# Second layer's v chunks: the low part of every second weight tile made by an adding DMA instead of VectorE

## Chip, cores and metric

The kernel runs on one core of a Trainium2 chip. The metric is the device time of one execution in microseconds (us), the median of several executions. Smaller is better.

## What is computed

A two-layer decoder trunk on 256 positions of width 2048, in float32. The first layer is attention with an output projection; the second is a gated unit. The change sits in the second layer, whose input projection is the wide one (2048 x 12288, cut into u, v and gate of 4096 columns each):

```python
def _odd_layer(x, ln_g, w_in, v_g, w_s, b_s, w_out):
    h = _rms(x, ln_g)
    z = h @ w_in
    uv = gelu(z[..., :2 * C_WIDTH])
    gate = silu(z[..., 2 * C_WIDTH:])
    u, v = uv[..., :C_WIDTH], uv[..., C_WIDTH:]
    v = _rms(v, v_g).reshape(Bn, S // C_CHUNK, C_CHUNK, C_GROUPS, C_GROUP_DIM)
    ws = w_s * tril(ones)
    s = einsum('gts,bnsgc->bntgc', ws, v) + b_s.T[:, :, None]
    return x + (u * s.reshape(Bn, S, C_WIDTH) * gate) @ w_out
```

## The kernel before

**Split products.** Every big product is done with numbers split into two parts of type fp32r: a high part (the value rounded) and a low part (the value minus its high part). A product a x w becomes three matmuls: high x high (line 121), high a x low w (line 122), low a x high w (line 123).

**Weight tiles.** `wtile` (lines 75 to 88) brings one weight tile of 128 x 2 x 512 float32 (512 KB, two k tiles of 128 rows, one chunk of 512 columns). SyncE issues the load into `wraw` (line 80, six buffers). ScalarE copies it to `whi` (line 85, four buffers), which rounds it. VectorE subtracts, `wlo` = `wraw` - `whi` (line 86, four buffers). A buffer of `whi` or `wlo` is free again when TensorE has done the last matmul that reads it, so the tile that stands four places later takes it.

**Chunks.** `gemm` (lines 100 to 126) computes one chunk of 512 output columns for both halves of the 256 positions. For the input projection of the second layer it goes through 16 k tiles in eight weight tiles (k0 = 0, 2, ..., 14), and does twelve matmuls of 512 columns with each of them: six into the PSUM bank of the first 128 positions, then six into that of the second.

**The v chunks.** Lines 557 to 566 run eight chunks, the columns 8 to 15 of `w_in1`. After each chunk ScalarE evacuates two banks with a Gelu (line 191, in `evac`) and sums squares of both halves (line 562, `junk`). GpSimd fetches a piece of the gain (line 564, `gv`) and multiplies it onto the chunk (line 565, `v`). The next chunk's matmuls don't wait for any of that. Afterwards the u and gate chunks follow.

**Order.** The framework orders each engine's instructions from the dependencies and its own estimate of when each is ready; instructions that stand earlier in the program go first among those that are ready. Each engine then runs its list strictly in that order and waits on semaphores where data isn't there yet.

Of the kernel before, what the change touches and what calls it, by code (L numbers as in the profile page):

```python
# [10 lines left out]
F32 = mybir.dt.float32  # L11
# [3 lines left out]
ALU = mybir.AluOpType  # L15
# [5 lines left out]
KT = D // P  # L21
# [12 lines left out]
def trunk(ctx, tc, x, xT, ev_g, w_in0, w_kva, qk_g, sinks, w_out0, od_g, w_in1, v_g, w_sT, b_s,  # L34
          w_out1, bias, badd, tri, out):
    nc = tc.nc
# [16 lines left out]
    def nm(s):  # L53
        uid[0] += 1
        return f"{s}{uid[0]}"

    def psum(tag, bufs):
        return ps.tile([P, 512], F32, tag=tag, bufs=bufs, name=nm(tag))
# [13 lines left out]
        return y  # L72


    def wtile(w, kt, cw, fine=False):
        raw = wpool.tile([P, 2, 512], F32, tag="wraw", bufs=6, name=nm("wraw"))
        src = w[kt // 2].rearrange("p (k n) -> p k n", k=2)
        step = 1 if fine else 2
        for j in range(0, 2, step):
            nc.sync.dma_start(raw[:, j:j + step, :cw], src[:, j:j + step, :])  # L80
        hi = wpool.tile([P, 2, 512], F32R, tag="whi", name=nm("whi"))
        lo = wpool.tile([P, 2, 512], F32R, tag="wlo", name=nm("wlo"))
        for j in range(0, 2, step):
            js = slice(j, j + step)
            nc.scalar.copy(hi[:, js, :cw], raw[:, js, :cw])  # L85
            nc.vector.tensor_tensor(lo[:, js, :cw], raw[:, js, :cw], hi[:, js, :cw].bitcast(F32),  # L86
                                    op=ALU.subtract)
        return hi, lo
# [3 lines left out]
    def fill():  # L92
        while fillers:
            try:
                next(fillers[0])
                return
            except StopIteration:
                fillers.pop(0)

    def gemm(aT, nkt, w, cw, pre=None, last=False):  # L100

        acc = [(psum("g", 4), 0, 0, cw), (psum("g", 4), 1, 0, cw // 2 if last else cw)]
        if last:
            acc.append((psum("g", 4), 1, cw // 2, cw))
        for k0 in range(0, nkt, 2):
            if pre is not None:
                pre(k0)
            fine = pre is not None and k0 == 0  # L110
            whi, wlo = wtile(w, k0, cw, fine)
            work = [(g, k) for g in acc for k in range(2)]
            if fine:
                work.sort(key=lambda t: t[1])
            for n, ((bank, tt, a, b), k) in enumerate(work):
                kt = k0 + k
                ah, al = aT(kt)
                sl = slice(tt * P, (tt + 1) * P)
                st, en = kt == 0, kt == nkt - 1
                o = bank[:, :b - a]  # L120
                nc.tensor.matmul(o, ah[:, sl], whi[:, k, a:b], start=st, stop=False)  # L121
                nc.tensor.matmul(o, ah[:, sl], wlo[:, k, a:b], start=False, stop=False)  # L122
                nc.tensor.matmul(o, al[:, sl], whi[:, k, a:b], start=False, stop=en)  # L123
                if n % 2:
                    fill()
        return acc if last else [g[0] for g in acc]
# [264 lines left out]
    def gate_y(q, y, gate):  # L391
# [3 lines left out]
        yield from split_T(y, yT0, q, [("t", 1)])  # L395

    in0 = lambda c, pre=None: gemm(hTk, KT, w_in0[c], 512, pre)

    acc = in0(QA, load_hT)
# [22 lines left out]
    zq1 = evac(accq, 512, rs=rs, name="qa")  # L422
    qk_norm(zq)
    acc1 = gemm(hTk, KT, w_kva, 256)
    qkg = cons.tile([P, 4], F32, name="qkg")
    nc.scalar.dma_start(qkg, qk_g)
# [70 lines left out]
    hT1 = [None] * 4  # L497
    ss1 = cons.tile([P, 2, 4], F32, name="ss1")

    def yTk(yT):  # L500
        def get(kt):
            while yT[kt // 4] is None:
                fill()
            return yT[kt // 4][0][:, kt % 4, :], yT[kt // 4][1][:, kt % 4, :]
        return get
# [29 lines left out]
    for q in range(4):  # L535
        acc = gemm(yTk(yT0), KT, w_out0[q], 512)
        resid(q, acc)
        fillers.append(next_hT(q))
# [12 lines left out]
        nc.gpsimd.tensor_tensor(t, t, trit.unsqueeze(1).broadcast_to([P, 8, P]), op=ALU.mult)  # L551
        ws.append(t)

    in1 = lambda c: gemm(yTk(hT1), KT, w_in1[c], 512)
    ssv = cons.tile([P, 2, 8], F32, name="ssv")
    vt = []
    for c in range(8):
# [132 lines left out]
```

## Time and profile before

| | |
|---|---|
| median of 3 runs | 1171.48 us (1170.75 to 1171.59) |
| the profiled execution | 1171.01 us |
| its span in the trace | 1169.2 us |
| TensorE busy in the span | 1162.0 us, 99% |
| VectorE busy | 647.5 us, 55% |
| ScalarE busy | 595.2 us, 51% |
| GpSimd busy | 135.7 us, 12% |
| DMA | 218.37 MB, mean 187 GB/s |

The trace has one row for each instruction: when it started, how long it ran, and what ended the idle time of its engine before it. PE is TensorE, ACT is ScalarE, DVE is VectorE, POOL is GpSimd, SP is SyncE, which issues most DMAs. A matmul's row is 0.39 us long, but matmuls overlap in the array: one starts every 0.227 us. The v chunks lie between about 449 and 625 us of the span.

### The profile page before, as it was taken

How to read it: one execution, taken by the hardware profiler on the slowest of the kernel's cores; microseconds unless marked ns; L12 is line 12 of the kernel's file. 1: busy time of each engine (PE TensorE's matmuls, PEld its weight loads, DVE VectorE, ACT ScalarE, POOL GpSimd, SP SyncE). 2: the span in 40 equal slices, each digit the busy share in tenths (PEclk: the TensorE clock that was granted, in tenths of full speed). 3: DMA queues.
4: the chain of work that ended last, by engine and by line, in shares of the span. 5: the costliest groups of instructions: out<-in, count | busy, mean ns of one | idle time of the engine just before them, and what ended most of it. 6: DMA issues, size and time to landing. Idle time of an engine off the chain costs nothing.

```text
span 1169.2 us, 14610 instructions
## 1 busy us (share of the span) xinstructions
PE 1162.0 (99%) x5546; PEld 963.0 (82%) x5546; DVE 647.5 (55%) x837; ACT 595.2 (51%) x818; POOL 135.7 (12%) x85
## 2 busy tenths in 40 slices
PE   9999999999999999999999999999999999999998
PEld 7887888788788888888888888888888888888887
DVE  6586556655645555554556555565556555454453
ACT  6556654544654544544545554555464455433332
POOL 0131111112103000211215110100000000000000
PEclk9999999999999999999999999999999999999999
DMA  9675335436436655666665555555555665566661
GB/s 349 232 245 195 127 108 184 172 109 208 160 123 219 196 186 183 203 212 200 202 213 178 184 188 190 181 178 187 186 187 171 190 187 173 198 215 199 200 213 37
DMA packets 63638, 218.37 MB, mean 187 GB/s; under 512 B 7632, under 2 KB 10320, under 8 KB 63312
## 3 DMA queue, kind: packets, MB, share of 16 engines
q1 hardware_dynamic: 60352, 209.74, 55.3%
q0 software_dynamic: 2080, 7.34, 2.0%
q8 instruction: 43, 0.70, 0.2%
q10 hardware_dynamic: 1136, 0.36, 0.1%
q14 instruction: 27, 0.22, 0.1%
HBM read 215.32 MB, written 2.10 MB: 186 GB/s over the span
## 4 chain that ended last, share of the span: by engine, by line
PE 96%; DVE 1%; POOL 1%; ACT 1%; DMA 0%; issue 0%; SPq 0%; ACTq 0%; POOLq 0%
PE g L121 30%; PE g L123 29%; PE g L122 29%; PE t L325 1%; POOL wsn L577 1%; PE s L296 1%; PE t L377 1%; PE s L299 1%; PE u L340 1%; PE u L341 1%; PE t L218 1%; PE u L339 1%; DVE wlo L86 0%; DMA wraw<-in_w_in_dram 0%; ACT whi L85 0%
## 5 line engine op out<-in xcount | busy, mean ns | idle before, releaser
L86 DVE TENSOR_TENSOR wlo<-wraw,whi 128x1024 fp32r<-128x1024 f32 (+1 forms) x393 | 514.0, 1312 | 427.3 <-ACT whi L85 426.5
L85 ACT CAST whi<-wraw 128x1024 fp32r<-128x1024 f32 (+1 forms) x393 | 409.1, 1043 | 480.9 <-PE g L123 457.1
L121 PE MATMUL g<-whi,hTh 128*128 128x512 f32 (+1 forms) x1184 | 464.6, 393 | 0.6 <-ACT whi L85 0.6
L122 PE MATMUL g<-wlo,hTh 128*128 128x512 f32 (+1 forms) x1184 | 458.9, 388 | 0.5 <-DVE wlo L86 0.5
L123 PE MATMUL g<-whi,hTl 128*128 128x512 f32 (+1 forms) x1184 | 459.4, 388 | 0.0
L121 PEld LDWEIGHTS g<-whi,hTh 128*128 128x128 f32 x1184 | 222.4, 188 | 45.2 <-ACT whi L85 1.0
L123 PEld LDWEIGHTS g<-whi,hTl 128*128 128x128 f32 x1184 | 222.5, 188 | 44.7
L122 PEld LDWEIGHTS g<-wlo,hTh 128*128 128x128 f32 x1184 | 222.7, 188 | 42.5 <-DVE wlo L86 1.0
L121 PE MATMUL g<-whi,yTh 128*128 128x512 f32 (+1 forms) x416 | 156.2, 375 | 0.0
L122 PE MATMUL g<-wlo,yTh 128*128 128x512 f32 (+1 forms) x416 | 155.3, 373 | 0.0
L123 PE MATMUL g<-whi,yTl 128*128 128x512 f32 (+1 forms) x416 | 155.2, 373 | 0.0
L123 PEld LDWEIGHTS g<-whi,yTl 128*128 128x128 f32 x416 | 78.3, 188 | 14.1
L122 PEld LDWEIGHTS g<-wlo,yTh 128*128 128x128 f32 x416 | 78.4, 188 | 13.5
L121 PEld LDWEIGHTS g<-whi,yTh 128*128 128x128 f32 x416 | 78.4, 188 | 13.6
L601 POOL TENSOR_TENSOR y<-y,gt 128x1024 f32<-128x1024 f32 x8 | 19.2, 2405 | 265.2 <-ACT gt L191 265.2
L565 POOL TENSOR_TENSOR v<-v,gv 128x1024 f32<-128x1024 f32 x8 | 21.9, 2743 | 220.2 <-ACT junk L562 220.2
L302 DVE CUSTOM_DVE_ANT_0 sb<-s,bias 128x256 f32<-128x256 f32 x32 | 13.5, 422 | 27.7 <-PE s L299 27.7
L577 POOL TENSOR_SCALAR wsn<-ws,rstdv 128x256 f32<-128x256 f32 x16 | 20.3, 1282 | 60.6 <-PE s L591 57.3
L191 ACT ACT_TABLE_LOAD x20 | 25.7, 1283 | 1.0 <-PE g L123 0.7
L315 ACT ACTIVATE pr<-sb,nmx 128x256 f32<-128x256 f32 x32 | 16.3, 510 | 18.9 <-DVE nmx L313 13.6
L272 POOL TENSOR_TENSOR bias<-bias,ba 128x1024 f32<-128x1024 f32 x8 | 20.8, 2598 | 33.9 <-DMA bias<-in_bias_dram 33.9
L583 DVE TENSOR_TENSOR vl<-v,vh 128x1024 fp32r<-128x1024 f32 x8 | 9.8, 1225 | 16.4 <-ACT vh L582 16.4
(130 smaller groups left out, 627.3 us busy)
## 6 DMA issues: line engine op xcount, KB each, us to landing
wraw<-in_w_in_dram SPq DMA_DIRECT2D x287, 512.0 KB, 3.7
wraw<-in_w_out_dram SPq DMA_DIRECT2D x96, 512.0 KB, 3.6
bias<-in_bias_dram POOLq DMA_DIRECT2D x8, 512.0 KB, 3.9
xT<-in_xT_dram SPq DMA_DIRECT2D x8, 256.0 KB, 5.1
xr<-in_x_dram SPq DMA_DIRECT2D x2, 1024.0 KB, 10.9
wraw<-in_w_kva_dram SPq DMA_DIRECT2D x8, 256.0 KB, 3.4
gv<-in_v_g_dram POOLq DMA_DIRECT2D x8, 256.0 KB, 3.1
out_dram<-o SPq DMA_DIRECT2D x7, 256.0 KB, 5.0
```

Of the source, the lines that this page charges most:

```text
L85: nc.scalar.copy(hi[:, js, :cw], raw[:, js, :cw])
L86: nc.vector.tensor_tensor(lo[:, js, :cw], raw[:, js, :cw], hi[:, js, :cw].bitcast(F32), op=ALU.subtract)
L121: nc.tensor.matmul(o, ah[:, sl], whi[:, k, a:b], start=st, stop=False)
L122: nc.tensor.matmul(o, ah[:, sl], wlo[:, k, a:b], start=False, stop=False)
L123: nc.tensor.matmul(o, al[:, sl], whi[:, k, a:b], start=False, stop=en)
L191: nc.scalar.activation(z[:, tt, :cw], acc[tt][:, :cw], func, scale=rs[:, tt:tt + 1])
L272: nc.gpsimd.tensor_tensor(bt, bt, ba[:, mix:mix + 1, :].broadcast_to([P, 4, 256]), op=ALU.add)
L302: nc.vector.tensor_tensor_reduce(out=sb[:, 0:256], in0=sp[:, 0:256], in1=bt[:, j, :], scale=1.0, scalar=NEG, op0=ALU.add, op1=ALU.max, acc ...
L315: nc.scalar.activation(pr[:, 0:256], sb[:, 0:256], AF.Exp, bias=nmx[:, j, 1:2], accum_out=l[:, j, 1:2])
L565: nc.gpsimd.tensor_tensor(v, v, gv.unsqueeze(1).broadcast_to([P, 2, 512]), op=ALU.mult)
L577: nc.gpsimd.tensor_scalar(wsn[:, n], ws[c // 4][:, (2 * c) % 8:(2 * c) % 8 + 2, :], rsv[:, n:n + 1], None, op0=ALU.mult)
L601: nc.gpsimd.tensor_tensor(y, y, gate[0], op=ALU.mult)
```

## The change

`wtile` gets a flag, `by_dma`. With it, VectorE's subtraction is left out. ScalarE writes minus the high part into `wlo` (one more instruction of the size of the copy), and GpSimd issues a DMA of 512 KB from `wraw` to `wlo`, inside SBUF, that adds what it reads onto what lies there. `gemm` sets the flag for tiles with k0 = 2, 6, 10 and 14, and only in the eight v chunks: 32 tiles, the odd ones of each chunk's tiles 0 to 7.

```diff
-    def wtile(w, kt, cw, fine=False):
+    def wtile(w, kt, cw, fine=False, by_dma=False):
@@
             nc.scalar.copy(hi[:, js, :cw], raw[:, js, :cw])
+            if by_dma:
+                nc.scalar.mul(lo[:, js, :cw], hi[:, js, :cw].bitcast(F32), -1.0)
+                nc.gpsimd.dma_start(lo[:, js, :cw], raw[:, js, :cw], accum_op=ALU.add)
+                continue
             nc.vector.tensor_tensor(lo[:, js, :cw], raw[:, js, :cw], hi[:, js, :cw].bitcast(F32),
                                     op=ALU.subtract)
@@
-    def gemm(aT, nkt, w, cw, pre=None, last=False):
+    def gemm(aT, nkt, w, cw, pre=None, last=False, by_dma=False):
@@
-            whi, wlo = wtile(w, k0, cw, fine)
+            whi, wlo = wtile(w, k0, cw, fine, by_dma and k0 % 4 == 2)
@@
-    in1 = lambda c: gemm(yTk(hT1), KT, w_in1[c], 512)
+    in1 = lambda c: gemm(yTk(hT1), KT, w_in1[c], 512, by_dma=c >= 8 and c < 16)
```

## Rows read from the trace of the kernel before

**Rows 1.** The page: busy time of TensorE, and granted clock in 40 slices.

```profile
PE 1162.0 (99%) x5546; PEld 963.0 (82%) x5546; DVE 647.5 (55%) x837; ACT 595.2 (51%) x818; POOL 135.7 (12%) x85
PEclk9999999999999999999999999999999999999999
```

**Rows 2.** Windows, the v stretch: length, busy PE PEld DVE ACT POOL, clock, DMA share, GB/s.

```profile
449.00:625.00 176.00, 176.00 (x780) 145.76 (x779) 90.44 (x84) 90.74 (x120) 23.55 (x15) 1.00 0.64 202
```

**Rows 3.** Waits of TensorE, whole span: waiter, releaser, us in total, times, longest.

```profile
PE t L218 <- ACT k L248: 1.0, 1, 1.0
...
PE g L122 <- DVE wlo L86: 0.5, 1, 0.5
```

**Rows 4.** Page, groups: line engine op xcount | busy, mean ns | idle before, releaser.

```profile
L86 DVE TENSOR_TENSOR wlo<-wraw,whi 128x1024 fp32r<-128x1024 f32 (+1 forms) x393 | 514.0, 1312 | 427.3 <-ACT whi L85 426.5
L85 ACT CAST whi<-wraw 128x1024 fp32r<-128x1024 f32 (+1 forms) x393 | 409.1, 1043 | 480.9 <-PE g L123 457.1
```

**Rows 5.** Timeline, TensorE, end of one v chunk: start, length, instruction.

```profile
512.65 0.39 PE L123 MATMUL g<-whi,hTl 128*128 128x512 f32 x1
512.88 0.39 PE L121 MATMUL g<-whi,hTh 128*128 128x512 f32 x1
...
515.60 0.39 PE L121 MATMUL g<-whi,hTh 128*128 128x512 f32 x1
...
518.32 0.39 PE L121 MATMUL g<-whi,hTh 128*128 128x512 f32 x1
...
521.04 0.39 PE L121 MATMUL g<-whi,hTh 128*128 128x512 f32 x1
521.27 0.39 PE L122 MATMUL g<-wlo,hTh 128*128 128x512 f32 x1
```

**Rows 6.** Timeline, ScalarE: two copies in a row, then the same chunk's end.

```profile
471.60 2.00 ACT L85 CAST whi<-wraw 128x1024 fp32r<-128x1024 f32 x2
...
510.36 1.06 ACT L85 CAST whi<-wraw 128x1024 fp32r<-128x1024 f32 x1 [1.66 <-PE g L123]
...
513.08 0.69 ACT L191 ACTIVATE v<-g,rstd 128x512 f32<-128x512 f32 x1
513.67 1.04 ACT L85 CAST whi<-wraw 128x1024 fp32r<-128x1024 f32 x1
514.61 0.63 ACT L562 ACTIVATE junk<-v 128x512 f32<-128x512 f32 x1
515.14 0.19 ACT L562 ACTIVATION_READ_ACCUMULATOR junk<-v 128x1 f32 x1
```

**Rows 7.** Timeline, GpSimd, the same chunk's end (the brackets: idle before, releaser).

```profile
515.42 2.81 POOL L565 TENSOR_TENSOR v<-v,gv 128x1024 f32<-128x1024 f32 x1 [18.40 <-ACT junk L562]
518.17 0.58 POOL L564 DMA_DIRECT2D gv<-in_v_g_dram  x1
```

**Rows 8.** The page, DMA issues: line engine op xcount, KB each, us to landing.

```profile
wraw<-in_w_in_dram SPq DMA_DIRECT2D x287, 512.0 KB, 3.7
...
bias<-in_bias_dram POOLq DMA_DIRECT2D x8, 512.0 KB, 3.9
...
gv<-in_v_g_dram POOLq DMA_DIRECT2D x8, 256.0 KB, 3.1
```

**Rows 9.** Line 271 alone, GpSimd's issue of `bias`: duration ns, min/median/max.

```profile
L271 POOL DMA_DIRECT2D bias<-in_bias_dram x8: 567/591/734, 71.8 to 293.9; - x8
...
DMA to landing us min/median/max: 3.8/3.9/7.9
```

**Rows 10.** Timeline, ScalarE, start of the first v chunk.

```profile
450.07 1.05 ACT L85 CAST whi<-wraw 128x1024 fp32r<-128x1024 f32 x1 [0.58 <-ACT hTh L527]
451.03 0.83 ACT L527 ACTIVATE hTh<-s,g 128x256 fp32r<-128x256 f32 x2
453.28 1.05 ACT L85 CAST whi<-wraw 128x1024 fp32r<-128x1024 f32 x1 [1.42 <-issue]
```

**Rows 11.** Waits of the DMA queue of SyncE, whole span.

```profile
SPq L80 <- DVE wlo L86: 862.1, 352, 11.2
```

## The prediction

> **What bounds the kernel now.** I read the page first: TensorE is busy for 1162.0 of 1169.2 us and its granted clock is in the top tenth in every slice [rows 1]. The reader should not stop at that share, because a busy row can hide waits. So I read the stretch that is changed: over the 176 us of the v chunks TensorE is busy for all 176.00 us at a granted clock of 1.00 (its upper level, 2.4 GHz), while VectorE, ScalarE and GpSimd have 90, 91 and 24 us of work there [rows 2]. The waits of TensorE over the whole span are single gaps of 1 us and less [rows 3]. TensorE alone sets the pace here, and relief of another engine has nothing to give back: 32 subtractions taken from VectorE are 32 x 1.23 us = 39 us of an engine that stands idle 427 us before this very line, waiting for `whi` [rows 4]. The question is only whether the new, longer way to `wlo` still arrives in time.
>
> **How much time there is.** I take the lead from one chunk's end. Tiles start on TensorE at 512.88, 515.60, 518.32 and 521.04, every 2.72 us [rows 5]. ScalarE's copy into `whi` is released by the end of a tile (idle time ended by `PE g L123`), and the copy at 510.36 [rows 6] belongs to the tile that starts at 518.32, since the buffer comes back four tiles later. The first matmul of a tile needs only `whi`; the second, 0.23 us on, needs `wlo` (521.04 and 521.27 for the next tile) [rows 5]. So from the start of the copy to the need of the low part there are 518.55 - 510.36 = 8.19 us.
>
> **Part 1: ScalarE writes minus the high part.** This trace has no such instruction in this size; the nearest row is the copy itself, 1.06 us alone and 2.00 us for two in a row [rows 6], so I take 1.00 us, 32 us in all. That stretch then has 91 + 32 = 123 us of ScalarE work in 176 [rows 2], hidden behind the matmuls; without that cover each would cost its 1.00 us. It can't cost less than nothing, since nothing on TensorE's path gets shorter. High part and negation together end 2.06 us after the start of the copy.
>
> **Part 2: GpSimd issues the adding DMA.** An issue of 512 KB from GpSimd takes 0.59 us of its sequence [rows 9], 32 x 0.59 = 19 us on an engine with 24 busy us of 176 [rows 2]. What lies behind it on GpSimd's queue when it waits for the negation is the multiplication of `v`, the fetch of `gv` and later adding DMAs. Nobody on TensorE's path needs `v` before the next part of the layer, so that direction costs nothing. The other direction does: the adding DMA can stand behind the multiplication of 2.81 us [rows 7].
>
> **Part 3: the transfer.** No row shows a DMA that adds, nor one inside SBUF. The nearest is a plain 512 KB load on the same GpSimd queue: 3.9 us from issue to landing in the median [rows 8], 3.8 at least and 7.9 at most [rows 9]. The adding one has to read two operands of 512 KB. What a further 512 KB costs on this queue follows from two rows: 256 KB land in 3.1 us and 512 KB in 3.9 [rows 8], 0.8 us for 256 KB more, so 5.5 us with the second operand. It also meets a DMA share of 0.64 from the weight loads [rows 2]. I take 5.9 us, the middle of 3.9 and 7.9 and near to 5.5, and keep 3.9 and 7.9 as the ends.
>
> On this the trace shows only that more bytes take longer [rows 8]. The Trainium skill (Collectives: The Full Stack, "The bandwidth ceiling: the fold count and why AG ≠ RS ≠ AR") says that an add in the DMA engines runs at half the rate of a copy because it reads two sources. No run here shows it yet; with 5.5 us by that rule in place of 5.9 the sum below would be 16.8 us and not 19.6.
>
> **Inside a chunk.** Issue at 2.06 us, so the transfer may take 8.19 - 2.06 = 6.13 us before TensorE waits. With 5.9 it is hidden by 0.2 us. Beyond 6.13 us every us costs: a buffer is refilled once in four tiles, and of the two buffers that take odd tiles the second gains what TensorE waited for the first, so a lateness of X is paid once per four tiles, 2X per chunk, 16X over eight chunks.
>
> **At the border of two chunks.** Here the cover is gone. Tile 7 of a chunk frees the buffer of tile 3 of the next, an odd one, so a changed one. The evacuation of the chunk goes first: the copy starts at 513.67, 0.59 us after its usual place at 513.08, then the sum of squares runs to 515.33 [rows 6], and the negation would end at 516.33. But the multiplication of `v` is released by that same sum of squares and holds GpSimd from 515.42; the next instruction there starts at 518.17 [rows 7]. It is older in the program and ready earlier, so I put the adding DMA behind it, and ahead of the `gv` fetch, which belongs to the end of the following chunk. Issue at 518.17, landing at 518.17 + 5.9 = 524.07, need at 521.27 [rows 5]: TensorE waits 2.80 us. Even the plain 3.9 us would be 0.80 late; the point from which it decides is 3.10 us, below the shortest landing of the nearest row, 3.8 [rows 9].
>
> There are seven such borders between v chunks. The first v chunk has none, since no multiplication precedes it; there the copy runs at 450.07 and two other ScalarE instructions to 451.86 [rows 10], negation to 452.86, landing at 458.76, and the need is 453.24 + 2 x 2.72 + 0.23 = 458.91 (the copy at 453.28 marks the end of its tile 0): hidden by 0.15 us. After the last v chunk the low parts come from VectorE again.
>
> **SyncE.** A `wraw` buffer is now freed by the landing of the adding DMA, not by VectorE. SyncE waits for VectorE in 352 of its loads, 862 us in all [rows 11], so loads are issued as buffers come free. A changed tile's buffer comes back at about the start of its own matmuls; the load for the tile six later has until the copy of that tile, three tiles or 8.16 us on, and takes 3.7 [rows 8]. The next load in SyncE's order has one tile more. I cost this at nothing; the cover is 4.5 us and goes if loads take over 8.
>
> **Sum.** 7 x 2.80 = 19.6 us. With the plain landing of 3.9 us it is 7 x 0.80 = 5.6. With 7.9 us, X is 1.77, and the border adds what it is later than usual, (518.17 - 513.08) - 2.06 = 3.03 us: 7 x 3.03 + 16 x 1.77 = 49.5. The profiled execution took 1171.0 us, 0.5 below the median of the runs. 1171.5 + 19.6 = 1191.1 us, with 1177 and 1221 as this case's own ends.
>
> **Rivals.** (1) *The adding DMA goes ahead of the multiplication* on GpSimd. For it: its negation ends 0.9 us after the multiplication becomes ready, and the order is fixed from estimates, not from these rows. Against: it is younger and later. Issue at 516.33, so 4.94 us are free at the border, 0.96 us late each, 7 x 0.96 = 6.7: 1178.2 us. (2) *Not slower.* The same order, and the transfer lands within 4.94 us; that is the point from which it decides. The plain 3.9 is inside, the 5.5 of two operands is not. Then nothing is late: 1171.5 us. (3) *The DMA engines become the bound.* They are at 0.64 with 202 GB/s [rows 2]; 512 KB in 5.44 us are 96 GB/s, 0.30 of a share if plain and 0.60 if paid twice, 1.24 together: 32 x 0.24 x 5.44 = 42 us, 1213. With queues that full landings pass 7.9 us: at 10 us, 7 x 3.03 + 16 x 3.87 = 83, 1255; at 12, 1287. Against it: the plain weight loads land in 3.7 us at this share. (4) *The clock.* Every window of before reads 1.00 and no wait of TensorE is longer than 1.0 us [rows 3], so no row shows what waits of 2.8 us do. If each were followed by one tile at the lower level, 1.2 GHz, that would be at most 2.72 us more, seven times 19: 1210. The Trainium skill (TensorE: Matmul & The Clock Gate, "What's actually happening") says that an engine that idles is throttled to the lower level. No wait here bears it out so far.
>
> Faster has no mechanism: TensorE's work is unchanged and it has no idle time in the stretch. Two per cent are for what I overlook.
>
> **How the numbers follow.** Forecast 0.55; adding DMA first 0.15; DMA engines or a slow adder (over 7.9 us) 0.15; clock 0.05; not slower 0.08; faster 0.02. What is left out of the range: not slower, faster, and landings over 10 us (half of the third rival), 0.18 together. Low: rival 1 with 5.5 us, 7 x 0.56 = 4, rounded down to 1174; high: 10 us, 1255. A measurement of this kernel can tell about 0.2% (2.3 us) from no change; beyond that lie all cases but the last two: slower 0.90, same 0.08, faster 0.02.
>
> **What would show it.** In the trace of after: seven waits of TensorE's line 122 on a DMA into `wlo`, some 2.8 us each, on tile 3 of v chunks 1 to 7, and none elsewhere in them; on GpSimd the adding DMA right behind line 565; its landings near 5.9 us; a granted clock of 1.00. Waits on all odd tiles would mean landings over 6.13 us. No wait at all would show that the order on GpSimd or the landing is not mine. Loads of `wraw` that TensorE or ScalarE wait for would show that SyncE's cover is gone.

## The result and the profile after

The changed kernel takes 1203.97 us (1201.1 to 1207.1, 4 runs), the kernel before 1171.24 (4 runs, the profiled one among them): a ratio of 1.028 (95% interval 1.026 to 1.030), 32.7 us slower. The forecast was 1191.1 us, slower, with a range of 1174 to 1255. The time lies in the range. The mechanism that carried the forecast, the place of the adding DMA behind a multiplication on GpSimd, was not the main one, as the rows below show. The adding transfers land too late, and the load on the DMA engines, the third rival's subject, makes them late.

The profiled execution is the longest of the four, 1207.1 us. First the page of the kernel after (span, busy time of the engines, granted clock and DMA share in 40 slices), against [rows 1]:

```profile
span 1204.9 us, 14692 instructions
PE 1175.4 (98%) x5546; PEld 967.8 (80%) x5546; DVE 608.6 (51%) x805; ACT 626.0 (52%) x850; POOL 161.6 (13%) x117
PEclk9999999999999999899999999999999999999999
DMA  9674436446346668999999565555565555566661
```

The moved work is where the diff puts it: VectorE loses 39 us, ScalarE gains 31, GpSimd 26. New are the nines in the DMA row in the slices of the v chunks (17 to 22) and one slice with a clock below the top. Windows (columns as in [rows 2]), first the v stretch, then what follows it:

```profile
449.00:660.00 211.00, 188.20 (x778) 149.59 (x777) 53.28 (x51) 121.43 (x150) 49.43 (x47) 0.96 0.92 250
660.00:1204.00 544.00, 541.03 (x2550) 452.88 (x2548) 287.78 (x275) 255.56 (x267) 42.27 (x25) 1.00 0.57 181
```

The v stretch ends at about 660 where it ended at about 625 [rows 2]. From the first squares of the residual to the last evacuation of `v` it takes 209.6 us against 174.1, so 35.5 of the 35.7 us by which the span grew lie in it. In the stretch the DMA share is 0.92 in place of 0.64 and TensorE waits. Its waits over the whole span, as in [rows 3]:

```profile
PE g L127 <- DMA wlo<-wraw: 22.7, 13, 3.0
PE t L141 <- DVE wz L136: 1.0, 1, 1.0
PE t L223 <- ACT k L253: 0.9, 1, 0.9
```

Thirteen waits, 22.7 us, on the landing of the adding transfer; line 127 is the former line 122. One of them in the timeline of TensorE, with the matmuls after it:

```profile
510.72 0.39 PE L126 MATMUL g<-whi,hTh 128*128 128x512 f32 x1
514.07 0.50 PE L127 MATMUL g<-wlo,hTh 128*128 128x512 f32 x1 [2.96 <-DMA wlo<-wraw]
514.40 0.39 PE L128 MATMUL g<-whi,hTl 128*128 128x512 f32 x1
...
516.13 0.63 PE L128 MATMUL g<-whi,hTl 128*128 128x512 f32 x1
516.56 0.63 PE L126 MATMUL g<-whi,hTh 128*128 128x512 f32 x1
516.99 0.63 PE L127 MATMUL g<-wlo,hTh 128*128 128x512 f32 x1
```

Some 1.6 us after the wait the distance from one matmul to the next goes from 0.23 to 0.43 us and the rows get longer: the granted clock is 0.50 there, its lower level, 1.2 GHz (a window, columns as in [rows 2]):

```profile
515.70:518.60 2.90, 2.90 (x8) 2.32 (x7) 0.00 (x0) 0.52 (x1) 0.00 (x0) 0.50 1.01 362
```

Four waits (2.1, 2.6, 3.0 and 2.9 us) were followed by such a stretch, two of them at once and two after 1.4 to 1.6 us; others (2.1, 2.3, 1.9 us) were not. The records show 33 distances of 0.43 us, 33 x 0.20 = 6.6 us. The wait of a row counts from the end of the matmul before it, and matmuls overlap; taken from start to start, beyond the usual 0.227 us, the thirteen waits cost 24.8 us. With the 6.6 us of the clock, and 3.7 us in other distances of over 0.3 us, half of them right behind a wait, that is 35.1 of 35.7 us.

The transfer itself, in the answer for its line 89 (GpSimd's issue, then from issue to landing), against [rows 8, 9]:

```profile
L89 POOL DMA_DIRECT2D wlo<-wraw x32: 856/866/926, 444.1 to 647.4; - x32
DMA to landing us min/median/max: 4.5/6.1/8.8
```

The median, 6.1 us, is near my 5.9. What I had not seen coming is the spread, up to 8.8, and where the long ones stand. The timeline of GpSimd and ScalarE around the border between the second and third v chunk, against [rows 6, 7]:

```profile
498.66 0.87 POOL L89 DMA_DIRECT2D wlo<-wraw  x1 [5.42 <-ACT wlo L88]
499.20 0.91 POOL L569 DMA_DIRECT2D gv<-in_v_g_dram  x1
...
502.28 1.04 ACT L86 CAST whi<-wraw 128x1024 fp32r<-128x1024 f32 x1
503.84 1.05 ACT L88 ACTIVATE wlo<-whi 128x1024 fp32r<-128x1024 f32 x1
...
505.18 0.86 POOL L89 DMA_DIRECT2D wlo<-wraw  x1 [5.08 <-ACT wlo L88]
506.60 2.73 POOL L570 TENSOR_TENSOR v<-v,gv 128x1024 f32<-128x1024 f32 x1 [0.56 <-DMA gv<-in_v_g_dram]
```

The adding DMA of tile 3 goes *ahead* of the multiplication of `v` (505.18 against 506.60), not behind it. It is late all the same, because it takes from 505.18 to 514.0, 8.8 us, to land. Only at the first border does the adding DMA stand behind the multiplication (477.33 to 479.73, issue at 479.69), and the negation had ended at 479.06, so it loses little by that.

### The profile page after: what moved, and what is told of

Same layout as the page of the kernel before. It is cut to its first block, busy times and chain, and to the rows that moved or that the text cites. A ratio compares the mean times of both kernels' runs of the same rounds, so it can differ in the third digit from the quotient of the medians.

```text
span 1204.9 us, 14692 instructions
## 1 busy us (share of the span) xinstructions
PE 1175.4 (98%) x5546; PEld 967.8 (80%) x5546; DVE 608.6 (51%) x805; ACT 626.0 (52%) x850; POOL 161.6 (13%) x117
## 3 DMA queue, kind: packets, MB, share of 16 engines
q0 software_dynamic: 6688, 24.12, 9.5%
## 4 chain that ended last, share of the span: by engine, by line
PE 86%; DMA 7%; ACT 3%; issue 1%; DVE 1%; POOL 1%; SPq 0%; POOLq 0%; ACTq 0%
PE g L127 26%; PE g L126 26%; PE g L128 26%; DMA wlo<-wraw 6%; PE t L330 1%; POOL wsn L582 1%; ACT whi L86 1%; PE s L301 1%; ACT wlo L88 1%; PE t L382 1%; PE s L304 1%; PE u L345 1%; PE u L346 1%; ACT v L196 1%; PE t L223 1%
## 5 line engine op out<-in xcount | busy, mean ns | idle before, releaser
L91 DVE TENSOR_TENSOR wlo<-wraw,whi 128x1024 fp32r<-128x1024 f32 (+1 forms) x361 | 475.3, 1320 | 501.5 <-ACT whi L86 500.9
L127 PE MATMUL g<-wlo,hTh 128*128 128x512 f32 (+1 forms) x1184 | 464.6, 392 | 23.3 <-DMA wlo<-wraw 22.7
L127 PEld LDWEIGHTS g<-wlo,yTh 128*128 128x128 f32 x416 | 78.4, 188 | 13.4
L89 POOL DMA_DIRECT2D wlo<-wraw x32 | 27.9, 870 | 220.5 <-ACT wlo L88 214.6
L88 ACT ACTIVATE wlo<-whi 128x1024 fp32r<-128x1024 f32 x32 | 33.8, 1057 | 0.8
## 6 DMA issues: line engine op xcount, KB each, us to landing
xr<-in_x_dram SPq DMA_DIRECT2D x2, 1024.0 KB, 10.9
```

Of the source, the lines that this page charges most:

```text
L88: nc.scalar.mul(lo[:, js, :cw], hi[:, js, :cw].bitcast(F32), -1.0)
L89: nc.gpsimd.dma_start(lo[:, js, :cw], raw[:, js, :cw], accum_op=ALU.add)
```

## The experiments

Two theories went in. A: the DMA engines; an adding transfer occupies them about twice as long as a plain one, and with the loads they can't keep TensorE's pace (the third rival). B: the place on GpSimd's queue at the border (the forecast). Besides, other causes were tried: the negation on ScalarE, the raw buffers that are held longer, the fetch of the gain. In the diffs, lines are those of the changed kernel.

**The negation alone.**

```diff
-                nc.gpsimd.dma_start(lo[:, js, :cw], raw[:, js, :cw], accum_op=ALU.add)
+                nc.vector.tensor_tensor(lo[:, js, :cw], raw[:, js, :cw],
+                                        lo[:, js, :cw].bitcast(F32), op=ALU.add)
```

> The negation on ScalarE stays, but VectorE adds the raw tile onto it in place of the DMA. All theories: ScalarE's 32 more instructions are hidden, 1171 to 1173 us. If the negation itself delays something, it shows here: over 1174.

Measured: 1171.82 us, ratio 1.0001 (0.9992 to 1.0011). ScalarE's 32 instructions are hidden, as Part 1 of the prediction had them, and the loss is all in the transfer.

**A plain transfer in place of the adding one.**

```diff
-                nc.gpsimd.dma_start(lo[:, js, :cw], raw[:, js, :cw], accum_op=ALU.add)
+                nc.gpsimd.dma_start(lo[:, js, :cw], raw[:, js, :cw])
```

> The transfer is made plain: it copies the raw tile and adds nothing, so this kernel leaves the subtraction out and multiplies with the raw tile in place of the low part. Theory A (the DMA engines: an adding transfer occupies them about twice as long as a plain one, 0.92 share in the v chunks, and landings reach 8 to 9 us where it meets the loads): share falls to about 0.80, landings to 4 to 4.5 us, time 1171 to 1178 us. Theory B (place on GpSimd's queue at the border, as predicted; the kind of transfer matters little): landings about 5, a wait of about 1 us at each border, 1180 us or more.

Measured: 1183.91 us, ratio 1.010 (1.008 to 1.013). About 12 us remain of 33, more than A gave, about what B gave; landings are 2.9 to 7.0 us, 4.8 in the median. The place is not B's: of the eight waits of TensorE (7.1 us) two are on tile 3 behind a border, some 0.7 us each, and six on tiles 5 and 7, whose transfers took 6.5 to 7.0 us. GpSimd's DMA queue on the page (packets, MB, share of 16 engines), first of the kernel before, then of this kernel, then of the kernel after:

```profile
q0 software_dynamic: 2080, 7.34, 2.0%
```

```profile
q0 software_dynamic: 6688, 24.12, 5.8%
```

```profile
q0 software_dynamic: 6688, 24.12, 9.5%
```

These rows are the price list. Before, this queue had 2080 packets and 2.0% of 16 engines' time in 1169.2 us; here it has 4608 packets more and 5.8% of 1180.1 us, after 9.5% of 1204.9. In engine time that is 721 us more for the plain transfers and 1457 us for the adding ones, over 16 engines and 32 transfers **1.41 and 2.85 us** each, a factor of about 2, with the same number of packets. That is the rule of the Trainium skill that the prediction weighed (Collectives: The Full Stack, "The bandwidth ceiling: the fold count and why AG ≠ RS ≠ AR"): an add reads two sources and runs at half the rate. Here the trace agrees. The 2.85 us hardly hang on the loads beside them: two kernels below, with half of the loads left out, give 2.87 and 2.90 in the same way (9.7% of 1188.1 us, 9.9% of 1173.0).

**What that does in throughput.** Before, the DMA engines are busy 0.64 of the v stretch [rows 2], 3.48 us for two tiles. With 2.85 us on top, two tiles ask for 6.33 us of DMA work in the 5.44 us that TensorE takes for them. 32 x 0.89 = 28.5 us is what the v chunks would get longer by this alone, an estimate. The stretch after gives less: the engines were busy for 0.92 of 211 us, 194 us, which is 18 more than the 176 that TensorE needs. That one of these numbers lies near the 32.7 us measured proves little: with the plain transfer two tiles ask for 4.89 us in 5.44, which is no excess, and 12 us were lost.

**The traffic beside the old way.** VectorE makes the low part, and the same transfers go into buffers that nobody reads.

```diff
-                nc.scalar.mul(lo[:, js, :cw], hi[:, js, :cw].bitcast(F32), -1.0)
-                nc.gpsimd.dma_start(lo[:, js, :cw], raw[:, js, :cw], accum_op=ALU.add)
-                continue
+                dm = c4([P, 2, 512], nm("dm"), F32R)
+                nc.scalar.mul(dm[:, js, :cw], hi[:, js, :cw].bitcast(F32), -1.0)
+                nc.gpsimd.dma_start(dm[:, js, :cw], raw[:, js, :cw], accum_op=ALU.add)
```

> The low part comes from VectorE as before, and beside it the same 32 negations and adding transfers go into buffers that nobody reads. Theory A in its latency form, and B: only TensorE's wait for the landing costs, so 1171 to 1174 us, with the DMA share at 0.9 or more. If the traffic itself hurts (loads late, TensorE waits for the high part): over 1176.

Measured: 1201.58 us, ratio 1.025 (1.023 to 1.027). TensorE needs none of these transfers and the loss is there in nearly full size. So it takes no wait of TensorE for the landing, and the picture in which only the lead of `wlo` counts falls. What TensorE and ScalarE wait for now (columns as in [rows 3]):

```profile
PE g L127 <- DVE wlo L91: 10.7, 13, 1.8
PE g L126 <- ACT whi L86: 6.7, 8, 2.4
...
ACT whi L86 <- DMA wraw<-in_w_in_dram: 76.8, 23, 11.1
```

The loss comes out at another place: ScalarE waits for raw tiles, since the transfers hold the raw buffers until they land. The place on GpSimd's queue isn't out of it. In this kernel the framework's order put the adding DMAs of tiles 3 and 5 behind the multiplication at six of the seven borders, and that of tile 3 left 4.8 to 8.6 us after its negation. One such border (timeline of ScalarE and GpSimd):

```profile
500.92 1.05 ACT L89 ACTIVATE dm<-whi 128x1024 fp32r<-128x1024 f32 x1
...
507.15 3.45 POOL L570 TENSOR_TENSOR v<-v,gv 128x1024 f32<-128x1024 f32 x1 [8.09 <-ACT whi L86]
510.56 2.65 POOL L90 DMA_DIRECT2D dm<-wraw  x3
...
523.60 1.04 ACT L86 CAST whi<-wraw 128x1024 fp32r<-128x1024 f32 x1 [11.06 <-DMA wraw<-in_w_in_dram]
```

The transfer was ready at 501.97, was issued at 510.56 and landed at 515.2, when SyncE issued its next load; that load took 8.3 us, and ScalarE's copy came right behind it. So there are three readings, which this run does not part: the DMA engines have too much to do, the raw buffers are held too long, or GpSimd issues too late.

**The same traffic without a hold on the raw buffers.** The transfers read the residual tile, which lies in SBUF anyway.

```diff
-                nc.gpsimd.dma_start(dm[:, js, :cw], raw[:, js, :cw], accum_op=ALU.add)
+                nc.gpsimd.dma_start(dm[:, js, :cw], xr[:, js, :cw], accum_op=ALU.add)
```

> As the kernel whose 32 negations and adding transfers go into buffers that nobody reads, but the transfers read the residual tile, which lies there anyway, in place of the raw weight tile: no weight buffer is held by them and TensorE waits for none. Throughput (an adding transfer takes the DMA engines 2.85 us, with 3.48 us of loads for two tiles that is 6.33 in 5.44): the loads come late all the same, 1190 to 1203 us. Coupling through the held raw buffers: 1171 to 1176 us.

Measured: 1193.65 us, ratio 1.018 (1.016 to 1.019). The time is that of the throughput theory; the way there is not the one I wrote. The traffic is the same in bytes only: the queue has 10784 packets in place of 6688, and a transfer takes 3.03 us of the engines, worked out as above. Up to 638 us of the span TensorE keeps its full pace, and the DMA engines have no room left (window, columns as in [rows 2]):

```profile
449.00:638.00 189.00, 189.00 (x837) 156.34 (x836) 95.01 (x97) 122.95 (x153) 56.21 (x43) 1.00 0.99 277
```

In the stretch the loads land in 8.3 us in the median where they took 4.2 before, which the raw buffers, free early again, still cover: TensorE waits for none of them. The adding transfers fall into arrears, 10.9 us in the median and up to 21.2, and the debt falls due at the end of the stretch, in one piece (timeline of GpSimd, ScalarE and TensorE):

```profile
651.36 2.33 POOL L570 TENSOR_TENSOR v<-v,gv 128x1024 f32<-128x1024 f32 x1 [7.87 <-DMA gv<-in_v_g_dram]
653.69 11.02 POOL L582 TENSOR_SCALAR wsn<-ws,rstdv 128x256 f32<-128x256 f32 x10
...
655.56 0.62 ACT L584 CAST wsh<-wsn 128x512 fp32r<-128x512 f32 x1 [26.91 <-POOL wsn L582]
656.08 1.04 ACT L86 CAST whi<-wraw 128x1024 fp32r<-128x1024 f32 x1
...
657.18 0.80 PE L126 MATMUL g<-whi,hTh 128*128 128x512 f32 x1 [18.74 <-ACT whi L86]
```

The fetch of the gain queues among the transfers, and the multiplications of `v` wait for it, 96 us in six waits; the adding DMAs behind them are issued up to 34 us after their negation. At the end the last multiplication waits for its fetch, ScalarE's next instruction waits for GpSimd, its copies stand behind it, and TensorE stops for 18.7 us. Arrears that had cost TensorE nothing during the v chunks cost nearly all at once. That the engines have no room at TensorE's pace is shown here; the size of the loss also hangs on GpSimd's list.

**One buffer more for the high and low parts.**

```diff
-        hi = wpool.tile([P, 2, 512], F32R, tag="whi", name=nm("whi"))
-        lo = wpool.tile([P, 2, 512], F32R, tag="wlo", name=nm("wlo"))
+        hi = wpool.tile([P, 2, 512], F32R, tag="whi", bufs=5, name=nm("whi"))
+        lo = wpool.tile([P, 2, 512], F32R, tag="wlo", bufs=5, name=nm("wlo"))
```

> All 32 transfers, but five buffers each for the high and the low parts (and one of the 26 four-KB buffers less): the lead grows by one tile, 2.72 us, from 6.1 to about 8.8 us for the landing. If the loss is latency (Theory A in its mild form, landings of 4.5 to 8.8 us against a lead of 6.1; also Theory B): 1171 to 1177 us. If the DMA engines are the bound in throughput (share 1.24 asked for), a fifth buffer can't help: 1195 to 1205 us.

Measured: 1195.91 us, ratio 1.021 (1.018 to 1.023). 2.72 us more of lead, which would cover nearly every landing of the kernel after, bring 8 of 33 us; 24 us stay, and the landings grow to 7.1 us in the median. By the expectation that speaks for throughput, but the trace shows that the order on GpSimd changed with the buffers. The adding DMA of tile 5 now stands behind the multiplication of `v` at all seven borders, and the multiplication behind the fetch of the gain (timeline of GpSimd, ScalarE and TensorE):

```profile
493.07 0.91 POOL L569 DMA_DIRECT2D gv<-in_v_g_dram  x1
...
496.68 1.06 ACT L88 ACTIVATE wlo<-whi 128x1024 fp32r<-128x1024 f32 x1
...
501.25 2.40 POOL L570 TENSOR_TENSOR v<-v,gv 128x1024 f32<-128x1024 f32 x1 [7.26 <-DMA gv<-in_v_g_dram]
503.60 1.76 POOL L89 DMA_DIRECT2D wlo<-wraw  x2
...
510.24 0.65 PE L127 MATMUL g<-wlo,hTh 128*128 128x512 f32 x1 [3.26 <-DMA wlo<-wraw]
```

The negation ends at 497.74, the DMA is issued at 503.60 and lands 6.6 us later. Six of TensorE's seven waits, 13.4 of 14.0 us, end on transfers that were issued 2.6 to 6.6 us after their negation in this way; in each of the six the delay on GpSimd was longer than the wait. So this run does not part throughput from latency: nearly all of its waits are of the forecast's kind, two tiles further on, with the gain's fetch made slow among the transfers (7.9 us in the median for 3.1 before [rows 8]).

**Half of the loads left out.** The even tiles of the v chunks all use one weight tile that stays (`held`).

```diff
+        raw = c4([P, 2, 512], nm("held")) if keep and not held else \
+            held[0] if keep else wpool.tile([P, 2, 512], F32, tag="wraw", bufs=6, name=nm("wraw"))
...
+            if not (keep and held):
+                nc.sync.dma_start(raw[:, j:j + step, :cw], src[:, j:j + step, :])
...
+            whi, wlo = wtile(w, k0, cw, fine, by_dma and k0 % 4 == 2, by_dma and k0 % 4 == 0)
```

> All 32 tiles go by the adding transfer, but the other 32 tiles of the v chunks all use one weight tile that stays in SBUF, so 31 loads are left out (and those products are with the wrong weights). Throughput: 1.74 + 2.85 = 4.6 us of DMA work in 5.44, landings 4.5 to 6: what is left is the border, mostly the first one, 1173 to 1183 us. If the loss is not the DMA engines' work: 1195 to 1205 us.

Measured: 1189.23 us, ratio 1.014 (1.013 to 1.016): half of the loss goes, not all. Neither theory's number. TensorE still waits 12.6 us in 13 waits of at most 1.6 us, with landings of 4.5 to 7.4 us around the lead of 6.1. GpSimd's order is that of the kernel after. The DMA engines have room here, 4.6 us of work in 5.44, so these 17 us are latency: landings that are longer than the lead.

**Both at once**, half of the loads and five buffers:

> Half of the loads left out (one weight tile that stays serves the even tiles, so those products are with the wrong weights) and five buffers for the high and the low parts, all 32 adding transfers. If the loss has just two parts, DMA work of 6.33 us in 5.44 and landings over the lead of 6.1 us, both are gone here (4.6 us of DMA work; landings up to 7.4 us against a lead of 8.8): 1171 to 1177 us. If something else delays TensorE: as with half the loads alone, 1185 to 1190 us.

Measured: 1179.67 us, ratio 1.007 (1.005 to 1.009). The profiled execution took 1174.84 us; the window of its v stretch, then the landings of the adding transfers:

```profile
455.00:628.00 173.00, 173.00 (x765) 143.11 (x764) 55.86 (x40) 118.03 (x144) 47.19 (x46) 1.00 0.86 209
```

```profile
DMA to landing us min/median/max: 4.5/5.5/7.6
```

TensorE is busy for all 173 us and waits for no adding transfer, though tile 5's is again issued 2.7 to 3.8 us after its negation at the borders: in this execution, the fastest of five, the 32 transfers run without a wait of TensorE in the stretch. Against the kernel with half of the loads alone, the longer lead brings 17 us down to 8 in the median; with a buffer more but all loads 24 stay, with neither 33. The other four executions took 1177 to 1183 us, and what they had more is not in this trace; that part stays open.

**The fetch of the gain and its multiplication left out**, both instructions of GpSimd at the border:

```diff
-        gv = m2([P, 512], nm("gv"))
-        nc.gpsimd.dma_start(gv, v_g[:, c * 512:(c + 1) * 512])
-        nc.gpsimd.tensor_tensor(v, v, gv.unsqueeze(1).broadcast_to([P, 2, 512]), op=ALU.mult)
```

> The fetch of the gain and its multiplication onto v are left out (so the v part lacks its gain); all 32 adding transfers stay. Theory A: 2 MB less on the DMA engines of some 60 in the stretch, a little shorter landings, 1192 to 1202 us. Theory B, or a contest of these two GpSimd instructions with the adding transfers for GpSimd and its queue: the waits at tiles 1 and 3 after each border go, 1175 to 1185 us.

Measured: 1198.14 us, ratio 1.022 (1.019 to 1.026). With no multiplication to stand behind, 26 of 33 us stay, and TensorE waits 17.9 us for landings of 4.6 to 8.6 us. This is the run that speaks against B in the kernel after, and the time is what A gave for 2 MB less.

**A seventh raw buffer** (`bufs=7` for `wraw`).

> One more buffer for the raw tiles (seven). If the loss comes from loads that SyncE must hold until an adding transfer frees a buffer, and that then come in a heap beside the next adding transfer: 1180 to 1195 us. If landings are long whatever the loads' order (Theory A) or by the place on GpSimd's queue (Theory B): 1198 to 1206 us.

Measured: 1203.04 us, ratio 1.027 (1.025 to 1.028). No gain that shows: SyncE's loads were not what was short in the kernel after, as the prediction had it.

**Half of the transfers, two choices.** `k0 % 8 == 2` in place of `k0 % 4 == 2`, then `k0 % 8 == 6`.

> Only tiles 1 and 5 of each v chunk take the new way (16 transfers, none of them the tile whose buffer is freed at a chunk's end). Theory A: share about 0.78, landings near 5 to 6 us, inside the lead of 6.1: 1171 to 1175 us. Theory B: no tile of the border is changed, 1171 to 1173 us.

Measured: 1174.47 us, ratio 1.002 (1.001 to 1.003). One wait of 0.8 us; the stretch from the first squares of the residual to the last evacuation of `v` is 175.9 us long against 174.1 before.

> Only tiles 3 and 7 (16 transfers, tile 3 is the one at the border). Theory A: as many transfers as with tiles 1 and 5, so nearly the same time, 1171 to 1178 us, landings near 5 to 6. Theory B: the seven waits at the borders stay, 2 to 3 us each: 1186 to 1192 us.

Measured: 1182.36 us, ratio 1.009 (1.007 to 1.011). The same traffic, 8 us more. Here the border does show: of the 6.0 us in three waits one is of 4.5, with a stretch of the lower clock behind it, on tile 3 of the second v chunk (timeline of ScalarE, GpSimd and TensorE):

```profile
469.23 1.28 ACT L196 ACT_TABLE_LOAD   x1
470.52 1.27 ACT L196 ACTIVATE v<-g,rstd 128x512 f32<-128x512 f32 x2
...
472.90 1.99 ACT L86 CAST whi<-wraw 128x1024 fp32r<-128x1024 f32 x2
473.09 2.40 POOL L570 TENSOR_TENSOR v<-v,gv 128x1024 f32<-128x1024 f32 x1 [9.14 <-ACT junk L567]
474.79 1.06 ACT L88 ACTIVATE wlo<-whi 128x1024 fp32r<-128x1024 f32 x1
...
476.15 0.88 POOL L89 DMA_DIRECT2D wlo<-wraw  x1 [0.66 <-ACT wlo L88]
...
483.95 0.63 PE L127 MATMUL g<-wlo,hTh 128*128 128x512 f32 x1 [4.50 <-DMA wlo<-wraw]
```

The multiplication is over at 475.49, before the negation ends at 475.85. So it is ScalarE that is late here, with a table load and two copies ahead of the negation, and the transfer then takes 7.8 us.

**Tiles 3 and 7 without that one transfer.**

> Tiles 3 and 7 as before (1182 us), but without tile 3 of the second v chunk, the only one whose adding transfer stands behind the multiplication of v on GpSimd's queue. If that place makes the loss (4.5 us of wait there and the clock after it): 1174 to 1177 us. If it is spread over the borders: 1180 us or more.

Measured: 1178.15 us, ratio 1.004 (1.003 to 1.006). One transfer of 16 is worth 4.2 us, about what its wait was. I had named GpSimd's queue as its cause in the expectation; the rows above name ScalarE's. The rest, 5.7 us, is above what I gave; TensorE's waits on the transfers are 2.1 us of it in the profiled execution, the remainder is not shown.

## Why the prediction was right, and where not

- **TensorE is the bound and VectorE's relief is worth nothing**: right. VectorE lost 39 us, and with the negation alone the time did not move.
- **Parts 1 and 2, the costs**: near. The negation took 1.06 us for my 1.00, the issue 0.87 us for 0.59 (the plain one 0.53).
- **Part 3, the landing**: the median, 6.1 for 5.9, was right and of little use. I took a constant from a queue that was nearly idle, and used a DMA share of 0.64 only to place a number between two ends. The term that was missing is the occupancy of the DMA engines: 2.85 us for each transfer, more than the 1.96 us in 5.44 that the loads left free. With it the share went to 0.92, and landings to as much as 8.8 us. The two operands, for which I took 0.8 us per 256 KB from two plain landings, were sized on the landing alone.
- **Inside a chunk**, "hidden by 0.2 us": wrong. Waits also stood at tiles 1, 5 and 7 in some chunks. The lead of 6.13 us was right: with half of the loads gone, landings of up to 7.4 us made waits of at most 1.6, and with a buffer more there were none in the trace.
- **At the border**, "behind the multiplication": this is the step that failed. The framework's order put the adding DMA first at six of seven borders. That was the first rival, to which I gave 0.15. Waits came about all the same on tile 3 behind six of the seven borders, 0.2 to 3.0 us where I had 2.80 for each, 12.6 of the 22.7 us. They come from landings of 5.0 to 8.8 us and from a part of the picture that was right: ScalarE's evacuation still goes first, so from issue to need there were 4.7 to 5.8 us at five of these borders and 2.8 at the first, where the first rival had 4.94. The other 10.1 us of waits, on tiles 1, 5 and 7, have no term in the sum.
- **SyncE**, at nothing: right.
- **The third rival**, DMA engines as the bound, names what makes the landings long, but is not the whole account. I had priced an adding transfer at 0.60 of share; it took 2.85 / 5.44 = 0.52, which turns 42 us into 28.5. That the engines have no room at TensorE's pace, the transfers from the residual tile show (0.99). That they need not be the bound for a loss, the plain transfers and the half of the loads show: 12 and 17 us with work for 0.90 and 0.85 of the time. How the 32.7 us divide between the two is not shown, since the run that was to part them changed GpSimd's order. I had argued against it with the plain loads' landing of 3.7 us, a median over the whole span that says nothing of how much room is left. In the v stretch it is 4.2 us before and 5.3 after.
- **The fourth rival**, the clock: it came in addition. Four of 13 waits were followed by the lower level, about 6.6 us, where I had 19 for seven. The Trainium skill (TensorE: Matmul & The Clock Gate, "What's actually happening") has an idle engine throttled to the lower level. The trace agrees for four waits of 2.1 to 3.0 us (granted clock 0.50 behind them), and not for two of 2.1 and 2.3 us, behind which it stays at 1.00.

So the sign and the range were right. The 19.6 us were the sum of a mechanism that mostly did not take place, and it is luck that they come within 13 us of the measured time: 1204 lies above the 1191 of the forecast and the 1178 of the first rival, and is in the range by the bounds that stand for slow landings.

## What to carry to other kernels

Before work goes from an engine to a DMA, add up the busy share of the DMA engines in that stretch and what the new transfers occupy, per tile and against the pace of the engine that bounds; an adding transfer counted twice here. A sum under one isn't enough: at 0.85 to 0.90 landings were still longer than the lead here, and 12 to 17 us were lost; at 0.85 a buffer more brought half of that back. A transfer that nobody waits for isn't free either: arrears in a shared queue come due at the next thing that stands in it. And look at the order of each engine in the trace of every experiment: one buffer more let the framework reorder GpSimd's list, and the run no longer tested what it was made for.

## What the runs showed of the hardware that was not expected

- A transfer of 512 KB that adds, SBUF onto SBUF, occupies the 16 DMA engines for 2.85 us, a plain one for 1.41, and lands in 6.1 against 4.8 us in the median beside the same loads.
- With the DMA engines busy for 0.98 of the v stretch, loads from SyncE landed in 8.3 us (median) and GpSimd's adding transfers in 10.9 on the same engines: both queues slowed, and TensorE waited for neither before the end of the stretch.
- The clock fell to its lower level behind single waits of 2.1 to 3.0 us in a TensorE that is otherwise full, at once or up to 1.6 us after it had resumed, and not behind two of 2.1 and 2.3 us.
